# Feed-forward products of a two-layer decoder step: seven block products in place of eight, with the activations kept in DRAM

## The chip, the cores and the metric

The kernel runs on one core of one Trainium2 chip. The metric is device time in microseconds (us) of one execution; smaller is better. TensorE (PE in the profile) multiplies matrices from on-chip memory (SBUF) into PSUM, VectorE (DVE), ScalarE (ACT) and GpSimd (POOL) work element by element, and SyncE (SP) issues most transfers. Each engine takes its own instructions in order.

## The reference

A prompt of 1024 tokens and a group of 64 sample tokens pass through two layers with shared weights, 1088 tokens of 1024 features. Layer 0 mixes tokens by retention and dilated attention, layer 1 by a state-space recurrence with a gated product (GLU). Each layer ends with the same feed-forward part, and that is where the change is made:

```python
def swiglu(h, w_in, w_out):                    # h [tokens, 1024], w_in [1024, 5632], w_out [2816, 1024]
    gate, up = jnp.split(h @ w_in, 2, axis=-1)
    return (jax.nn.silu(gate) * up) @ w_out
...
        yp = yp + swiglu(rms_norm(yp, norm_ffn[layer]), w_ffn_in[layer], w_ffn_out[layer])
```

All arrays are float32.

## The kernel before

Features lie on partitions and tokens along the free dimension, in T = 1092 columns (1088 tokens and 4 empty ones), cut into three parts of CH = 364. Every large product is exact to about float32 by three products of a shortened format: each operand is split into a high part (`split_a`, `split_w`, `w_unit`: an ACT copy) and a low part (a DVE subtraction), and `mm_fm` (line 169 of the profile) adds hi*hi, lo*hi and hi*lo. One output block of 128 features with 8 blocks of input features is 8 x 3 x 3 = 72 matmuls.

`ffn(l, ...)` runs once per layer. It scales and splits the residual `x` into `hh` and `hl`, without the norm's factor; the factor `rb` is multiplied onto the results. Then, for each of the NF = 22 blocks of 128 hidden features, it makes the gate product (72 matmuls), L1223 to L1225 (times the factor, SiLU, times the factor), the up product (72 matmuls), L1234 (the gated activation `a`) and its split. After each pair of blocks `out_proj` multiplies the pair before by its rows of `w_out`: 8 groups of 18 matmuls, each added to `x` by DVE (L1207). So the second product runs between the pieces of the first one, `x` stays in SBUF throughout, and an activation lives only until its pair is used. The last pair is left to `turn_over`: `s5_start` in layer 0, which prepares the state-space layer between the output blocks, and `final` in layer 1, which works by columns of tokens and normalizes the result.

Weights come in units of 256 columns (`w_raw`, 1 MB each, two buffers `raw`).

Beside layer 0's feed-forward runs background work for the state-space layer, `s5_prep2`, a generator of which `ffn` takes 8 steps per block (`next(bgen, None)`). It has 32 passes `hd` of two groups; each is some 30 POOL instructions (L1021 to L1065) with transposes on PE (L1074, L1084), copies on DVE (L1013) and, every fourth pass, a chain of small DVE and ACT instructions (`phases`, L851). Its memory is the pool `prep`, opened above the split activations and held until `eh.close()`. In layer 1 the background is `caches`: sixteen copies of 4080 KB from DRAM to DRAM, issued by POOL.

From the attention on, everything stands in one block whose order on each engine is set when the program is built, by a planner that runs through the instructions on a simulated device (`tc.block(schedule_with_timeline_sim=True)`); the engines then take that order as it is.

## Time and profile before

| what | us |
|---|---|
| median of 3 runs (lowest to highest) | 2705.1 (2701.85 to 2706.35) |
| span of the profiled execution | 2704.3 |
| layer 0's feed-forward, first to last matmul (743.3 to 1579.2) | 835.9 |
| layer 1's feed-forward up to the last gate and up product (1891.1 to 2660.6) | 769.5 |
| PE busy in the whole span | 2630.6 (97%) |

The times of the runs are of the device. The span is from the first to the last instruction of the one execution that was profiled; it lies inside the range of the timed runs, so what stands around it in the timed figure is within a microsecond or two. Busy PE time says that a matmul was under way, not that PE ran at its best rate: the rate is read from how many matmuls a stretch of time holds.

### The profile page before, as it was taken

How to read it: one execution, taken by the hardware profiler on the slowest of the kernel's cores; microseconds unless marked ns; L12 is line 12 of the kernel's file. 1: busy time of each engine (PE TensorE's matmuls, PEld its weight loads, DVE VectorE, ACT ScalarE, POOL GpSimd, SP SyncE). 2: the span in 40 equal slices, each digit the busy share in tenths (PEclk: the TensorE clock that was granted, in tenths of full speed). 3: DMA queues.
4: the chain of work that ended last, by engine and by line, in shares of the span. 5: the costliest groups of instructions: out<-in, count | busy, mean ns of one | idle time of the engine just before them, and what ended most of it. 6: DMA issues, size and time to landing. Idle time of an engine off the chain costs nothing.

```text
span 2704.3 us, 43413 instructions
## 1 busy us (share of the span) xinstructions
PE 2630.6 (97%) x17493; PEld 2514.5 (93%) x17493; DVE 1178.8 (44%) x2224; ACT 739.9 (27%) x1283; POOL 702.1 (26%) x1337
## 2 busy tenths in 40 slices
PE   7999999999999999999999988999999999999998
PEld 7997788778999999999999987999999999999998
DVE  6223333965554444344434368532433333333325
ACT  5113344764232111122111175321311111111112
POOL 2000022431026765666670044300100000000003
PEclk9999999989999999999999999999999999999999
DMA  8337852314133322223326199411565546431001
GB/s 238 121 101 258 289 202 73 83 40 140 59 80 91 92 74 74 71 79 88 88 70 114 50 289 250 140 57 38 173 231 171 169 143 216 156 109 47 32 32 75
DMA packets 258153, 331.52 MB, mean 123 GB/s; under 512 B 59697, under 2 KB 223441, under 8 KB 256673
## 3 DMA queue, kind: packets, MB, share of 16 engines
q1 hardware_dynamic: 254896, 255.58, 31.9%
q0 software_dynamic: 3056, 73.17, 7.9%
q8 instruction: 138, 2.26, 0.4%
q14 instruction: 63, 0.51, 0.1%
HBM read 270.06 MB, written 129.66 MB: 148 GB/s over the span
## 4 chain that ended last, share of the span: by engine, by line
PE 85%; DMA 6%; DVE 5%; ACT 2%; issue 1%; SPq 1%; POOL 1%; DVEq 0%; POOLq 0%; ACTq 0%
PE big L169 64%; PE ch L308 7%; PE ch L215 2%; PE po L729 1%; DMA x_d<-x 1%; DMA kv<-in_state_swa_k 1%; PE tr L718 1%; PE tr L367 1%; PE po L409 1%; DMA U<-h_d 1%; PE sc L702 1%; PE sm L169 1%; DMA out_swa_v_prompt<-v_ev 1%; PE pb L1561 1%; PE sc L374 1%
## 5 line engine op out<-in xcount | busy, mean ns | idle before, releaser
L169 PE MATMUL big<-hh,wh_i 128*128 128x364 f32 (+1 forms) x2080 | 461.4, 329 | 0.9 <-DVE sg L1223 0.9
L169 PE MATMUL big<-hh,wl_i 128*128 128x364 f32 (+1 forms) x2080 | 460.1, 328 | 0.0
L169 PE MATMUL big<-hl,wh_i 128*128 128x364 f32 (+1 forms) x2080 | 458.6, 327 | 0.0
L169 PEld LDWEIGHTS big<-hh,wl_i 128*128 128x128 f32 x2080 | 361.6, 188 | 0.1
L169 PEld LDWEIGHTS big<-hh,wh_i 128*128 128x128 f32 x2080 | 359.5, 188 | 2.3 <-DVE sg L1223 1.2
L169 PEld LDWEIGHTS big<-hl,wh_i 128*128 128x128 f32 x2080 | 358.5, 188 | 0.1
L790 ACT ACTIVATE wh_i<-raw 128x1024 fp32r<-128x1024 f32 x111 | 117.7, 1060 | 868.2 <-PE big L169 825.2
L1207 DVE TENSOR_TENSOR x<-big,x 128x1092 f32<-128x1092 f32 x168 | 217.1, 1293 | 204.4 <-PE big L169 204.4
L1225 POOL TENSOR_TENSOR sg<-sg,ssq 128x1092 f32<-128x1092 f32 x21 | 53.4, 2541 | 806.1 <-ACT sg L1224 806.1
L169 PE MATMUL big<-a_hi,wh_o 128*128 128x364 f32 x1008 | 225.8, 332 | 6.3 <-DVE a L1234 3.5
L169 PE MATMUL big<-a_hi,wl_o 128*128 128x364 f32 (+1 forms) x1008 | 222.8, 329 | 0.0
L169 PE MATMUL big<-a_lo,wh_o 128*128 128x364 f32 (+1 forms) x1008 | 222.1, 328 | 0.0
L1223 DVE TENSOR_TENSOR sg<-big,ssq 128x1092 f32<-128x1092 f32 x44 | 57.0, 1295 | 341.7 <-PE big L169 339.1
L1234 DVE TENSOR_TENSOR a<-big,sg 128x1092 f32<-128x1092 f32 x42 | 54.4, 1295 | 324.8 <-PE big L169 320.9
L169 PEld LDWEIGHTS big<-a_hi,wh_o 128*128 128x128 f32 x1008 | 171.9, 188 | 11.1 <-DVE a L1234 4.1
L169 PEld LDWEIGHTS big<-a_lo,wh_o 128*128 128x128 f32 x1008 | 176.1, 188 | 0.0
L169 PEld LDWEIGHTS big<-a_hi,wl_o 128*128 128x128 f32 x1008 | 174.7, 188 | 0.3 <-issue 0.2
L791 DVE TENSOR_TENSOR wl_i<-raw,wh_i 128x1024 fp32r<-128x1024 f32 x109 | 137.1, 1258 | 50.7 <-ACT wh_i L790 50.7
L126 ACT ACTIVATE wh_o<-raw 128x1024 fp32r<-128x1024 f32 x44 | 46.4, 1060 | 323.9 <-PE big L169 310.7
L308 PE MATMUL ch<-h_hi,wh_a 128*128 128x364 f32 (+1 forms) x384 | 129.3, 337 | 0.3 <-ACT wh_a L121 0.3
L308 PE MATMUL ch<-h_lo,wh_a 128*128 128x364 f32 (+1 forms) x384 | 128.8, 335 | 0.0
L308 PE MATMUL ch<-h_hi,wl_a 128*128 128x364 f32 (+1 forms) x384 | 128.3, 335 | 0.0
(556 smaller groups left out, 4535.1 us busy)
## 6 DMA issues: line engine op xcount, KB each, us to landing
raw<-in_w_ffn_in SPq DMA_DIRECT2D x44, 1024.0 KB
out_swa_k_sample<-in_state_swa_k POOLq DMA_DIRECT2D x8, 4080.0 KB, 15.6
out_swa_v_sample<-in_state_swa_v POOLq DMA_DIRECT2D x8, 4080.0 KB, 15.8
raw<-in_w_ffn_out SPq DMA_DIRECT2D x22, 1024.0 KB
kv<-in_state_swa_k SPq DMA_DIRECT2D x40, 512.0 KB
kv<-in_state_swa_v SPq DMA_DIRECT2D x40, 512.0 KB
raw<-in_w_in_ab SPq DMA_DIRECT2D x24, 512.0 KB
tb<-sc_all SPq DMA_DIRECT2D x16, 642.0 KB
```

The source lines that it names most:

```text
L126: S.activation(hi, src, AF.Copy)
L169: last = PE.matmul(pc[c][:, :n], lhsT=w(k), rhs=a(k, c)[:, :n], start=j == 0, stop=j == K * 3 - 1)
L215: PE.matmul(pv[:n, :256], lhsT=a[:, k, tk], rhs=w[:, k % 4, :], start=j == 0, stop=j == 23)
L308: PE.matmul(pb[:, :n], lhsT=w[:, k], rhs=a[:, k, c * CH:c * CH + n], start=j == 0, stop=j == 23)
L367: PE.transpose(pt[:, hp], kn[:, hp * 128:(hp + 1) * 128], ident)
L374: PE.matmul(ps_[hp * 32:hp * 32 + 32, :w], lhsT=qs[:, hp, b], rhs=kt[:, hp, :w], start=True, stop=True)
L790: S.activation(hi, r, AF.Copy)
L791: split_ins[0] = (eng or V).tensor_tensor(lo, r, f32(hi), op=OP.subtract)
L1207: V.tensor_tensor(c3(x[:, m]), pb[:, :, :CH], c3(x[:, m]), op=OP.add)
L1223: V.tensor_tensor(c3(sg), pg[:, :, :CH], c3(rb), op=OP.mult)
L1225: last_op = (G if l and f < NF - 1 else V).tensor_tensor(sg, sg, rb, op=OP.mult)
L1234: V.tensor_tensor(c3(a), pu[:, :, :CH], c3(sg), op=OP.mult)
```

## The change

The first product is computed by Strassen's scheme, in Winograd's form. A unit is 1024 input features by 256 weight columns. Its weights are a 2 x 2 block matrix (512 x 128 each), and so are the activations (512 features by HT = 544 tokens). Seven products of sums of blocks replace eight products of blocks, for every one of the 44 units per call (22 in each layer). A product is 4 blocks of features x 3 terms x 2 parts of QC = 272 columns = 24 matmuls.

What this moves around it:

- The norm's factor is applied to the activations before the product, so their sums can be formed once per layer; `x` is used up for it and goes to DRAM (`x_d`) before, in halves of tokens, and is loaded again for the second product. The products ahead of each feed-forward part (three of the output projection, the last of the GLU) are done in halves of tokens (`mm_half`), with the norm's sums between them.
- Each unit forms its weight sums and seven splits on DVE and ACT. Results are put together from PSUM by DVE.
- All 22 blocks of gated activations go to DRAM (`a_d`) and come back for the second product, which now follows the whole first one: `out_proj(0, 8)`, `out_proj(8, 15)`, and the rest in `turn_over`.
- Background steps: 8 per unit instead of 8 per block of gate and up.

The core of the diff:

```diff
+    class Halves:      # PSUM: two banks "sm", and either 2 tiles of three banks (big) or 3 of two (pair)
...
+        hc = eh.enter_context(tc.tile_pool(name="ffh", bufs=1, reuse_waits="tile"))
+        H = {}
+        for nm in ("S2", "S3", "S1", "A22", "S4", "A12", "A11"):
+            H[nm] = [hc.tile([128, 4, HT], F32R, name="%s_%s" % (nm, pt)) for pt in ("hi", "lo")]
+        def put(nm, k, src, eng):
+            hi, lo = H[nm]
+            S.activation(hi[:, k], src, AF.Copy)
+            eng.tensor_tensor(lo[:, k], src, f32(hi[:, k]), op=OP.subtract)
+        E = G if l else V
+        class Unit:
+            def split(self, nm, src, hilo=None):
+                hi, lo = hilo or [w4.tile([128, 4, 128], F32R, name=n) for n in ("wh_p", "wl_p")]
+                S.activation(hi, src, AF.Copy)
+                V.tensor_tensor(lo, src, f32(hi), op=OP.subtract)
+            def weights(self, nm):
+                sub = lambda o, a, b: V.tensor_tensor(o, a, b, op=OP.subtract)
+                if nm == "S2":
+                    sub(b11, b12, b11)
+                    self.t2 = tp[0].tile([128, 4, 128], F32, name="t2", bufs=1)
+                    sub(self.t2, b22, b11)
+                elif nm == "S3":
+                    sub(b12, b22, b12)
+                elif nm == "A22":
+                    sub(b21, b21, self.t2)
+                self.split(nm, ...)
+            def prod(self, nm):
+                    for k in range(4):
+                        for w, a in ((hi, ah), (lo, ah), (hi, al)):
+                            for c in range(2):
+                                last = PE.matmul(ps[:, c, :QC], lhsT=w[:, k], rhs=a[:, k, c * QC:(c + 1) * QC], ...)
+            def put(self, j, hf, a, b):
+                if not self.up:
+                    V.tensor_tensor(o, a, b, op=OP.add)
+                    S.activation(o, o, AF.Silu)
+                else:
+                    V.tensor_tensor(t, a, b, op=OP.add)
+                    bgen_after[0] = E.tensor_tensor(o, t, o, op=OP.mult)
+            def m1(self): ...  # A11, copied by ACT     def m2: A12, put    def m6: S2, u2 = p + m1
+            def m7(self): ...  # S3, u3 = p + u2        def m5: S1, u2 = p + u2, put    def m4: A22, put   def m3: S4, put
...
+        def norm(o, k, hf, eng):
+            S.activation(o, o, AF.Identity, scale=g[:, k:k + 1])
+            eng.tensor_tensor(o, o, ssq[:, half(hf)], op=OP.mult)
+        for k in range(4):
+            norm(blk[k][0], k, 0, V)
+            put("A11", k, blk[k][0], V)
...
+        for k in range(4):
+            norm(blk[k][1], k + 4, 0, V)
+            put("A12", k, blk[k][1], G)
...
+        for k, (a11, a12, a21, a22) in enumerate(blk):
+            norm(a21, k, 1, G)
+            norm(a22, k + 4, 1, V)
+        for k, (a11, a12, a21, a22) in enumerate(blk):
+            V.tensor_tensor(q1[k], a21, a22, op=OP.add)
+            G.tensor_tensor(a21, a11, a21, op=OP.subtract)
+            V.tensor_tensor(a11, q1[k], a11, op=OP.subtract)
+            put("S2", k, a11, V)
+        ... # put S3 (G), S1 (V), A22 (V); a12 - a11 (G), put S4 (G)
-        for gi in range(NG):
-            ... # gate, up and, per pair, out_proj
+        for gi in range(NG):
+            for u in (gate unit, up unit):
+                u.m1(); u.m6(); u.m2(); u.m7(); u.m5(); u.m4(); u.m3()
+                if bgen_after[0] or not l:
+                    bg_step(8)
+            pending.append(lambda sg=sg, gi=gi: [SP.dma_start(a_d[:, gi * 2 + j], sg[:, j]) for j in range(2)])
+        for _ in bgen:
+            pass
+        eh.close()
+        def load_a(f, slot):
+            ... # memory of ffw (slots 0 to 5), zp (6, 7), ffw2 (from 8)
+            SP.dma_start(lo[:, :NT], a_d[:, f])
+            G.memset(lo[:, NT:], 0.0)
+            S.activation(hi, lo, AF.Copy)
+            V.tensor_tensor(lr, lo, f32(hi), op=OP.subtract)
+        def out_proj(f0, f1, hook=None):
+            for m in range(KT):
+                wv = w_unit(raw, m % 2, n=f1 - f0)
+                mm_fm(pb, wv, f1 - f0, ...)
+                V.tensor_tensor(c3(x[:, m]), pb[:, :, :CH], c3(x[:, m]), op=OP.add)
+        for f in range(8):
+            load_a(f, f)
+        x = x_tile(xr)
+        for m in range(KT):
+            SP.dma_start(x[:, m], x_d[:, m])
+        f2 = e2.enter_context(tc.tile_pool(name="ffw2", bufs=1, reuse_waits="tile"))
+        for f in range(8, 15):
+            load_a(f, f)
+        out_proj(0, 8)
+        for f in range(15, NF):
+            load_a(f, f - 15)
+        out_proj(8, 15)
+        turn_over(fp, zp, out_proj, outs, acts)
```

Pools of the changed kernel are opened with `reuse_waits="tile"`: a tile waits for the tiles that lay in its place, not for the whole pool. By the tiles' sizes, per partition: the seven splits `H` take 122 KB from the bottom of the pool stack, `prep` lies above them; `ffw`, `zp` and `ffw2` take 131 KB from the same bottom, so that the low parts of blocks 12 to 14 (the top of `ffw2`) lie where `prep` lay.

## Rows read from the trace of the kernel before

**Rows 1.** Windows: us of the stretch, busy us per engine (instructions), granted clock, DMA share

```profile
743.30:1579.20 835.90, 827.36 (x5054) 807.86 (x5054) 359.72 (x448) 179.11 (x269) 438.61 (x1010) 1.00 0.32 87
1891.10:2660.60 769.50, 768.57 (x4646) 768.11 (x4644) 271.75 (x223) 126.60 (x119) 61.26 (x37) 1.00 0.39 130
759.90:1435.80 675.90, 668.89 (x4098) 650.16 (x4097) 287.94 (x379) 135.39 (x225) 420.97 (x992) 1.00 0.29 82
1925.00:2000.00 75.00, 75.00 (x454) 75.00 (x454) 1.00 0.81 270
```

**Rows 2.** PE's waits in layer 0's feed-forward: line, releaser, total us, times, longest

```profile
PE big L169 <- DVE a L1234: 3.5, 2, 2.0
PE sm L1105 <- DMA Ex<-in_state_ssm_im: 1.5, 2, 0.8
```

**Rows 3.** Critical chain, in order of time: start us, us, what

```profile
391.48 23.70 PE ch L215 x198
...
851.59 24.08 PE big L169 x144
...
1669.98 6.43 DMA hz<-z_d
```

**Rows 4.** Lines L272, L1207, L790: durations in ns, min/median/max, and shapes

```profile
L272 DVE TENSOR_TENSOR h_lo<-g,h_hi x9: 431/683/1678, 7.7 to 49.4; 128x512 fp32r<-128x512 f32 x8, 128x272 fp32r<-128x272 f32 x1
L1207 DVE TENSOR_TENSOR x<-big,x x168: 1281/1295/1297, 830.4 to 2643.8; 128x1092 f32<-128x1092 f32 x168
L790 ACT ACTIVATE wh_i<-raw x111: 1041/1062/1066, 643.6 to 2613.1; 128x1024 fp32r<-128x1024 f32 x111
```

**Rows 5.** Line L1225: durations in ns on DVE and on POOL

```profile
L1225 DVE TENSOR_TENSOR sg<-sg,ssq x23: 1283/1328/2254, 773.2 to 2659.2; 128x1092 f32<-128x1092 f32 x23
L1225 POOL TENSOR_TENSOR sg<-sg,ssq x21: 2540/2540/2543, 1922.8 to 2603.7; 128x1092 f32<-128x1092 f32 x21
```

**Rows 6.** Timeline at 889 us, and line L1062 on POOL in ns

```profile
889.48 3.64 POOL L1021 TENSOR_TENSOR u<-Cc,tA 128x144 f32<-128x144 f32 x4
...
889.60 1.39 DVE L791 TENSOR_TENSOR wl_i<-raw,wh_i 128x1024 fp32r<-128x1024 f32 x1
...
890.92 1.52 DVE L1225 TENSOR_TENSOR sg<-sg,ssq 128x1092 f32<-128x1092 f32 x1
...
L1062 POOL TENSOR_TENSOR u<-tE x128: 394/407/1456, 805.7 to 1410.3; 128x128 f32<-128x128 f32 x128
```

**Rows 7.** DVE groups in layer 0's loop (742 to 1510 us): busy us, mean ns

```profile
L791 DVE TENSOR_TENSOR wl_i<-raw,wh_i 128x1024 fp32r<-128x1024 f32 x43 | 56.9, 1323 | 0.3 <-ACT wh_i L790 0.3
L1225 DVE TENSOR_TENSOR sg<-sg,ssq 128x1092 f32<-128x1092 f32 x21 | 29.4, 1400 | 0.5
L127 DVE TENSOR_TENSOR a_lo<-a,a_hi 128x1092 fp32r<-128x1092 f32 x21 | 29.0, 1381 | 6.8 <-ACT a_hi L126 6.7
L127 DVE TENSOR_TENSOR wl_o<-raw,wh_o 128x1024 fp32r<-128x1024 f32 x20 | 25.8, 1294 | 19.4 <-ACT wh_o L126 19.4
```

**Rows 8.** POOL's waits in layer 0's loop: total us, times, longest

```profile
POOL u L1021 <- DVE u L851: 78.2, 7, 20.5
POOL Bp L1036 <- PE sm L1084: 65.3, 7, 18.1
POOL u L1021 <- DVE Cc L1013: 26.5, 3, 13.8
POOL Bp L1036 <- DMA B<-in_ssm_b_im: 15.7, 2, 8.6
```

More of the change, by code (lines that the diff above doesn't have):

```diff
@@ L22 @@
 T = 3 * CH
+HT = NT // 2
+QC = HT // 2
 TP = 1152
@@ new lines, in behind, with norm_stats, norm_rows @@
+    def behind(ins):
+        return tc.issue_after(ins.ins) if ins is not None else ExitStack()
+    def norm_stats(pool, hf, after=None):
+        pr = psX.sm()
+        with behind(after):
+            for i, o in enumerate((0, 128, 256, 384, HT - 128)):
+                last = PE.matmul(pr[:, i:i + 1], lhsT=ssq[:, hf * HT + o:hf * HT + o + 128], rhs=ones, start=True, stop=True)
+        return rstd_newton(pool, pr[:, :5]), last
+    def norm_rows(r, hf, after=None):
+        pa, pb = psX.sm(), psX.sm()
+        with behind(after):
+            for i in range(4):
+                PE.matmul(pa[:, i * 128:(i + 1) * 128], lhsT=r[:, i:i + 1].to_broadcast([128, 128]), rhs=ident, start=True, stop=True)
+            last = PE.matmul(pb[:, :HT - 512], lhsT=r[:, 4:5].to_broadcast([128, 128]), rhs=ident[:, 640 - HT:], start=True, stop=True)
+        S.activation(ssq[:, hf * HT:hf * HT + 512], pa, AF.Copy)
+        S.activation(ssq[:, hf * HT + 512:(hf + 1) * HT], pb[:, :HT - 512], AF.Copy)
+        return last
@@ new lines, in mm_half @@
+    def mm_half(ps, wv, K, ah, al, after=None, mid=None):
+        hi, lo = wv
+        terms = [(w, a, k) for k in range(K) for w, a in ((hi, ah), (lo, ah), (hi, al))]
+        for j, (w, a, k) in enumerate(terms):
+            if mid and j == K * 3 // 2:
+                after = mid(last)
+            with behind(after):
+                for c in range(2):
+                    r = a(k, c)
+                    o = ps[:, c, :QC]
+                    if len(r.shape) == 3:
+                        o = o.rearrange("p (s c) -> p s c", s=8)
+                    last = PE.matmul(o, lhsT=w(k), rhs=r, start=j == 0, stop=j == K * 3 - 1)
+        return last
@@ L1171, in step_kernel @@
             pass
+        raws = first_raws(0)
+        pe = None
+        for hf in range(2):
+            for j, wv in enumerate(last):
+                m = 5 + j
+                pb = psX.big()
+                o = hf * HT
+                pe = mm_half(pb, wv, KT, lambda k, c: m_hi[:, k, o + c * QC:o + (c + 1) * QC], lambda k, c: m_lo[:, k, o + c * QC:o + (c + 1) * QC], pe)
+                if hf and j == 0:
+                    r0, pe = norm_stats(xP, 0, pe)
+                elif hf and j == 1:
+                    pe = norm_rows(r0, 0, pe)
+                xv = x[:, m, half(hf)].rearrange("p (c n) -> p c n", c=2)
+                V.tensor_tensor(xv, pb[:, :2, :QC], xv, op=OP.add)
+                save_half(tC, m, hf)
@@ new lines, in ffn @@
+        t1, t2 = half(0), half(1)
+        g = gains["ffn%d" % l]
+        blk = [[x[:, k + d, t] for t in (t1, t2) for d in (0, 4)] for k in range(4)]
+        def norm(o, k, hf, eng):
[4 more added lines that the diff above has]
+            put("A11", k, blk[k][0], V)
+        first = Unit(0, None, False, raws[0])
+        first.after = first_after
@@ new lines, in ffn @@
+        first.split("A11", first.block(0, 0), [s1.tile([128, 4, 128], F32R, name=n, bufs=1) for n in ("wh_s", "wl_s")])
+        first.m1s = s1.tile([128, 2, QC], F32, name="m1", bufs=1)
+        first.m1()
+        r1, first.after = norm_stats(xP, 1, first.after)
+        first.split("A12", first.block(1, 0), [wU.tile([128, 8, 128], F32R, name=n)[:, :4] for n in ("wh_i", "wl_i")])
+        for k in range(4):
+            norm(blk[k][1], k + 4, 0, V)
+            put("A12", k, blk[k][1], G)
+        p2 = first.prod("A12")
@@ new lines, in ffn @@
+        first.after = norm_rows(r1, 1, first.after)
+        q1 = [s1.tile([128, HT], F32, name="q1") for k in range(2)]
+        q1 += [ssq[:, hf] for hf in (t1, t2)]
+        for k, (a11, a12, a21, a22) in enumerate(blk):
[6 more added lines that the diff above has]
+            put("S2", k, a11, V)
@@ L1324, in hook @@
                     load_t(i)
-        out_proj((NF - 2, NF - 1), hook)
+        out_proj(15, NF, hook)
     U, tabs = {}, {}
```

350 lines of the change are left out of this document (245 added, 105 removed).

## The prediction

> **What bounds the kernel now.** I read the page's busy shares first, then windows over the two feed-forward parts, then the chain of waits inside them. In both parts PE is the limit: it is busy 827.4 of 835.9 us in layer 0 and 768.6 of 769.5 us in layer 1, at the full clock (1.00), while DVE has work for 360 and 272 us and POOL for 439 and 61 us [rows 1]. PE's longest wait for another engine in layer 0 is 2.0 us [rows 2]. So what counts is how long PE takes per matmul. A busy share can't tell that, but a piece of the chain without waits can: 144 matmuls of 364, 364 and 360 columns take 24.08 us, 0.1672 us each, and 198 of 256 columns, every one with new weights, take 23.70 us, 0.1197 us each [rows 3]. The reader is to see that the price goes nearly by columns; the narrower matmul isn't bound by its weight load.
>
> **What the change takes from PE.** Before, a layer's first product is 44 outputs x 72 = 3168 matmuls x 0.1672 = 529.7 us. After, it is 22 units x 7 products x 24 = 3696 matmuls of 272 columns. No row has that width; on the line between the two prices of [rows 3] (0.0475 us for 106.7 columns) it is 0.1268 us, so 468.7 us. The gain is 61.0 us a layer. Bounds: the price of 256 columns (442 us, gain 87), and that price enlarged by 272/256 (470 us, gain 60). I take the line, since 272 lies next to 256. The second product keeps its matmuls: 22 x 72 = 1584 x 0.1672 = 264.8 us, of which 240.8 (20 of 22 blocks) lie in layer 1's window. Check: layer 1 before is 3168 + 1440 = 4608 x 0.1672 = 770 against 769.5 [rows 1]. In layer 0 835.9 - 529.7 - 264.8 leaves 41.4 us: 8.5 us idle, and 33 us of matmuls for the background and the norm, which stay. The five outputs that are now made in halves cost 96 x 0.1268 = 12.2 in place of 12.0 us each, 1 us together.
>
> **What it adds to the other engines.** A subtraction of 512 elements took DVE 0.683 us, one of 1092 from PSUM 1.295 us [rows 4]; on that line 544 elements take 0.72 us. A unit gives DVE 4 weight sums and 7 low parts (11 x 0.683 = 7.5 us), 7 additions from PSUM (5.0 us) and, in layer 0's up units, 4 multiplications (2.9 us): 14.0 us on average per unit, against 168 x 0.1268 = 21.3 us of PE. ACT has 7 high parts at about half of 1.062 us [rows 4], one copy and half the time four SiLUs, about 6 us. Neither is the limit by load, and three PSUM pairs and four weight buffers stand between them and PE. DVE loses 64 of its 88 additions to `x` a layer, hidden before and after.
>
> **Start of each part.** Formerly PE began as soon as one block was split. Now the norm's factor, the sums and seven splits come first. POOL has 24 instructions of 544 elements; scaled from 2.540 us for 1092 [rows 5] each takes 1.27 us, 30.5 us in all. DVE has 36 instructions with both operands in SBUF beside them, and these two kinds don't run together (next part): 36 x (0.72 - 0.2) us, three quarters of them met, add 14 us, so 44 us until S4 is split. PE can do eight products before it needs S4 (A11 and A12 of gate and up, then S2, S3, S1, A22): 24.3 us. That leaves a stall of 20 us per layer; 8 if four products of the up unit go ahead of S4, 32 if the chain starts 12 us late. I take 20.
>
> **Between the products.** Blocks 0 to 7 must come back before `out_proj(0, 8)`. Their memory is that of S2, S3 and S1, which the last unit uses up first, so the loads (6.43 us for 544 KB [rows 3]) can begin some 9 us before its end; what isn't covered is the last additions from PSUM and the split of the first `w_out` block. Bounds 0 and one load with its split, 6.4 + 1.1 + 1.3 = 8.8 us; I take 4. The DRAM traffic itself (12 MB out, 12 MB back, `x` twice 4.5 MB, a layer) lies beside PE at DMA shares of 0.32 and 0.39 [rows 1]. In layer 1 sixteen copies now come one per unit: 4.18 MB + 1.05 MB of weights + 0.56 MB of activations in 21.3 us is 272 GB/s, what a stretch of before carried at a share of 0.81 without holding PE (75.00 of 75 us busy) [rows 1]. I cost it at nothing; if it isn't covered, a weight unit comes late in layer 1 alone.
>
> **Layer 0's background, the term that decides.** When POOL and a DVE instruction with two SBUF operands meet, one waits for the other: at 889 us L791 takes 1.39 us and L1225 1.52 while four POOL instructions take 3.64 us [rows 6]; the DVE groups of this kind run 0.1 us over their undisturbed 1.215 and 1.296 us [rows 7]; L1062 takes 0.407 us in the middle and 1.456 at most [rows 6]. So a meeting costs POOL 1.05 us for an instruction of 1.25: its length less 0.2. (The Trainium skill, SBUF — State Buffer, section "SBUF: two separate sides", calls it an exclusive lock, held for the whole instruction. By whole lengths the delay worked out below would be 140 in place of 99 us and the forecast 2698; the rows show 0.2 us less per meeting.)
>
> Before, the background ran 675.9 us with POOL busy 421 [rows 1]. In it lie waits on PE's order and on loads, 65.3 + 26.5 + 15.7 = 107.5 us [rows 8], and 105 DVE instructions of the kind [rows 7], met with a chance of 421/676, at 1.05 us: 68 us. Without these it is 500 us, 71% of it POOL work; the chains of small instructions (78.2 us [rows 8]) are in it. After, a unit has 11 + 2 such DVE instructions, 8.9 us, which cost 13 x 0.2 less, 6.35 us; 22 units x 6.35 x 0.71 = 99 us. POOL begins 45 us after the start of the part. So the background ends 45 + 500 + 99 + 5 (the second product's splits) = 649 us after the start, though eight steps per unit ask it to be done in 20 units.
>
> Who waits for that? The low parts of blocks 12 to 14 lie in `prep`'s place, and `out_proj(8, 15)` wants them first at 20 + 468.7 + 33 + 10 (DVE late here and there, since POOL now delays it too) + 4 + 96.3 (`out_proj(0, 8)`, 576 matmuls) + 6 = 638 us. They can be there at 649 + 8.8 = 658. PE is held 20 us.
>
> **The sum.** Layer 0: 468.7 + 264.8 + 33 + 20 + 10 + 4 + 20 = 820.5, against 835.9: -15.4. Layer 1: 468.7 + 240.8 + 2 (norm) + 20 + 4 = 735.5, against 769.5: -34.0. With +1: -48 from 2704.3, and 0.8 up to the median: **2657 us**.
>
> **Rivals.**
> (1) The background doesn't hold PE, and the start is covered (8 and 2 us in place of 20 and 4): layer 0 776.5, layer 1 721.5, together -106: 2600. For it: POOL's 107 us of waiting show that it isn't pressed now [rows 8]. Against it: two passes per unit want 2 x 500/32 = 31 us of a unit of 21.
> (2) Slower: PE's order is fixed when the program is built. Its background transposes (L1074, L1084), and SP's stores of POOL's results, stand in that order at the times that the planner gave POOL. If it gave POOL none of the 99 us of meetings, PE and, through weight loads queued behind those stores, its units wait for them within the first product: 2657 + 99 - 20 = 2736. At worst each of 16 units takes two full passes (31 + 4.5 us in place of 22.8): 2657 + 16 x 13 - 20 = 2845. It decides from 48 us, 3 us per unit. For it: POOL is oversubscribed in the new first product even without meetings. Against: before, PE waited for the background 1.5 us in all [rows 2].
> (3) DVE paces the units: 14.0 us of work plus 13 x 0.1 of meetings and some 1.5 of background copies is 79% of a unit in layer 0, in a fixed order, with evictions and next weights in one queue. One to one and a half us uncovered in each of 44 units: 2701 to 2723. Against: in layer 1 its load is 60%.
>
> **How the numbers follow.** The forecast's case has 0.45 (2635 to 2690), rival 1 0.25 (2585 to 2635), rival 2 0.18, rival 3 0.12. A measurement of this kernel tells about 0.2%, 5.4 us, from no change. Faster: 0.45 + 0.25 + half of rival 3 = 0.76; the same: most of the rest of rival 3 and a tail of rival 2, 0.07; slower 0.17. The range goes from 2590 (rival 1 but for its lower end) to 2725 (rival 3 whole, rival 2 left out from there).
>
> **What would show it.** In the changed profile: the first product's matmuls start 0.127 us apart where PE doesn't wait, and 3696 of them a layer; a gap of PE of some 20 us in all within the first 60 us of each feed-forward part, ended by POOL's S3 or S4; the last POOL instruction of the background near 650 us after layer 0's start, and the load of block 12 behind it; DVE waits of 0.1 to 0.3 us per instruction in layer 0 and nearly none in layer 1; layer 1 gaining about twice what layer 0 gains. Wrong would be: PE waiting unit by unit for background or weights (rivals 2, 3), or layers that gain alike (rival 1). The forecast fails most easily in the 500 us of background, from which small changes go into PE's hold one to one.

## The result, and the profile after

The changed kernel takes 2845.4 us (median of 4, 2839.1 to 2848.4), the kernel before 2703.5 beside it (4, 2698.0 to 2706.4): a ratio of 1.053, 95% interval 1.051 to 1.055. It is slower by 142 us, where 48 us less were forecast. Its profiled span is 2837.3 us, 133.0 more than before.

Windows of the changed kernel, columns as in [rows 1], the last one GB/s. In each layer: the first unit (with 20 matmuls of the norm's sums in it); the other 21; the time to the first matmul of the second product; the second product, in layer 0 in two rows (297.0 us together).

```profile
741.30:811.50 70.20, 30.03 (x189) 28.95 (x189) 57.19 (x69) 20.60 (x35) 36.74 (x24) 0.64 0.04 5
811.50:1336.00 524.50, 490.26 (x3754) 469.94 (x3752) 341.64 (x597) 156.75 (x318) 388.01 (x853) 0.98 0.36 107
1336.00:1347.00 11.00, 2.02 (x15) 0.81 (x14) 4.49 (x6) 3.39 (x4) 10.57 (x30) 0.76 0.86 278
1347.00:1451.00 104.00, 97.68 (x561) 94.36 (x562) 27.28 (x22) 18.64 (x29) 56.53 (x128) 0.94 0.71 176
1451.00:1644.00 193.00, 184.92 (x1085) 182.89 (x1084) 56.71 (x48) 50.71 (x49) 15.11 (x20) 0.97 0.49 143
1968.20:2034.10 65.90, 28.89 (x188) 27.81 (x189) 53.03 (x60) 21.33 (x35) 36.14 (x22) 0.68 0.19 65
2034.10:2532.40 498.30, 451.20 (x3530) 450.12 (x3528) 261.85 (x373) 128.91 (x207) 75.56 (x64) 0.95 0.59 204
2532.40:2538.70 6.30, 0.29 (x4) 0.07 (x2) 4.17 (x4) 3.12 (x3) 1.59 (x9) 0.81 0.93 301
2538.70:2795.50 256.80, 244.05 (x1440) 242.89 (x1441) 80.97 (x69) 45.20 (x45) 0.71 (x7) 0.97 0.28 102
```

Against [rows 1], layer 0 takes 902.7 us (741.3 to 1644.0) where it took 835.9, and layer 1 827.3 where it took 769.5. 12 us more lie ahead of layer 1's first matmul, 4 less elsewhere. PE, formerly busy for 99% of layer 0, now stands still or runs at 1.2 GHz at every change of stage.

What a unit costs when nothing stops it is read from experiment e3 below, where layer 1's last 21 units run without a wait:

```profile
2135.30:2578.20 442.90, 442.90 (x3530) 442.88 (x3528) 262.35 (x373) 129.89 (x207) 74.38 (x57) 1.00 0.46 162
```

442.9 / 3528 = 0.1255 us per matmul of 272 columns, 21.09 us per unit; 22 units are 464 us, where the eight products took 529.7. So the scheme gives PE its 65.7 us a layer, and the rest of the stage takes that and 67 or 58 us more. By the prediction's own terms:

| layer 0 | forecast | measured |
|---|---|---|
| 22 units | 468.7 | 464.0 |
| second product and background on PE | 264.8 + 33 | 264.8 + 33 (taken as forecast) |
| start of the part | 20 | 49.1 (70.2 - 21.1) |
| units held | 10 | 57 (524.5 - 442.9 - 25 for 226 of the background's matmuls) |
| between the products | 4 | 11.0 |
| held before blocks 8 to 14 | 20 | 8 |
| loads, background and clock in the second product | 0 | 16 (297.0 - 264.8 - 8 of background - 8) |

| layer 1 | forecast | measured |
|---|---|---|
| 22 units, norm | 470.7 | 464.0 (the norm's 2 stand in the start) |
| second product, 20 blocks | 240.8 | 240.8 |
| start of the part | 20 | 44.8 (65.9 - 21.1), and 12 ahead of it |
| units held | 0 | 55.4 (498.3 - 442.9) |
| between the products | 4 | 6.3 |
| loads late in the second product | 0 | 16.0 (256.8 - 240.8) |

The 25 us are an estimate: 33 us for 302 matmuls in the kernel before, in proportion. In e10 below, where PE hardly waits, its units take 36 us more than 442.9 for 221 matmuls of the background. So of the 57 us 34 are PE's waits (524.5 - 490.3), some 11 the clock, and some 12 the background's own matmuls, which cost more between units than the 25 (11 and 12 go by e10).

The hold of 8 us is PE's wait of 7.2 us at 1465.7 us, ahead of the first product with `f_hi`, and 0.9 behind it. Three terms make most of the loss: the starts, layer 0's units, layer 1's units. PE's waits show each. In the names below, `wh_p` and `wl_p` are the high and the low part of a sum of weights; Sx, Ox and Ex are tables that POOL makes for the background (Cs is one that it loads), and PE transposes or multiplies them (L1118, L1181, L1191). In the two starts (732 to 812 us and 1955 to 2035 us; 35.4 us in each, 4.3 ahead of layer 0's first product, 12.0 ahead of layer 1's):

```profile
PE pp L1377 <- ACT wh_p L1350: 35.4, 1, 35.4
PE pp L1377 <- ACT wh_s L1350: 4.3, 1, 4.3
...
PE pp L1377 <- ACT wh_s L1350: 12.0, 1, 12.0
```

After four products PE waits 35.4 us for S2's weight. The timeline shows what DVE and POOL do then (DVE's first two lines, then POOL's):

```profile
771.12 1.84 DVE L1458 TENSOR_TENSOR ssq<-x,x 128x544 f32<-128x544 f32 x1
772.89 0.71 DVE L1333 TENSOR_TENSOR A_lo<-x,A_hi 128x544 fp32r<-128x544 f32 x1
...
768.87 1.75 POOL L1459 TENSOR_TENSOR x<-x 128x544 f32<-128x544 f32 x1 [0.66 <-DVE q L1458]
770.58 1.81 POOL L1333 TENSOR_TENSOR S_lo<-x,S_hi 128x544 fp32r<-128x544 f32 x1
```

Here they take turns: a DVE instruction of 0.71 us takes 1.84 when it meets one of POOL, and POOL's take 1.75 to 1.81 where the shortest of this shape took 1.33 (L1397 in layer 1). POOL's 24 instructions of the start take 41.5 us in all, meetings included. But POOL waits too (735 to 798 us):

```profile
POOL x L1435 <- ACT ssq L898: 13.4, 1, 13.4
POOL x L1459 <- DVE q L1458: 3.2, 2, 2.5
POOL x L1468 <- DVE x L1460: 2.0, 2, 1.3
POOL x L1459 <- DVE ssq L1458: 0.7, 1, 0.7
```

The 13.4 us (14.6 in layer 1) are for the norm's factor of the second half of the tokens: the matmuls of its sums stand behind PE's first product, at 751 us, and the factor is there at 757, 15.8 us after PE's first matmul. The last low part of S4 is out at 797.0 us, 55.7 after that matmul, and the chain runs to 798, 57 after it. Its last link is the weight sum `t2`, whose place lies in `x`, and so behind the last low part of S4:

```profile
795.74 1.80 DVE L1356 TENSOR_TENSOR t<-raw 128x512 f32<-128x512 f32 x1 [1.88 <-POOL S_lo L1333]
```

PE then goes on at half clock (windows, granted clock third from the end):

```profile
790.00:798.00 8.00, 0.00 (x0) 0.00 (x0) 6.12 (x5) 4.99 (x8) 7.00 (x5) 0.50 0.00 0
798.00:802.00 4.00, 2.75 (x10) 2.44 (x11) 4.00 (x8) 1.77 (x4) 0.00 (x0) 0.50 0.00 0
802.00:806.00 4.00, 4.00 (x21) 4.00 (x20) 1.58 (x3) 0.54 (x1) 0.00 (x0) 0.53 0.00 0
806.00:810.00 4.00, 4.00 (x35) 4.00 (x34) 3.41 (x10) 0.73 (x2) 0.28 (x2) 1.00 0.45 44
```

So a wait costs more than its length: in layer 0's first unit PE is busy for 30.0 us with what takes 21.1 at full clock and with the norm's sums, some 2 us, so some 7 us go to the clock. The 49.1 us are thus 40.2 of waits (35.4, and the rest mostly for low parts of weights), 7 of clock and 2 of the norm.

In layer 0's other units PE waits for the background in its own order (811 to 1336 us), 1.5 us in all before [rows 2]; these are the two largest:

```profile
PE sm L1181 <- POOL Sx L1131: 24.7, 14, 4.0
PE sm L1191 <- POOL Ox L1131: 5.0, 5, 1.6
```

In layer 1's other units PE waits 47.1 us in all (2034 to 2533 us), in two stretches: 14 us between 2095 and 2135 us, half of them for DVE, and 32.9 from 2285 to 2318 for the high part of a weight sum, whose load took from 2274.4 to 2317.8:

```profile
PE pp L1377 <- ACT wh_p L1350: 39.4, 2, 32.9
PE pp L1377 <- DVE sg L1392: 7.7, 1, 7.7
```

POOL's timeline before the first stretch, the critical chain there, and a window:

```profile
2057.99 0.55 POOL L1869 DMA_DIRECT2D out_swa_v_sample<-in_state_swa_v  x1
2058.53 0.50 POOL L1869 DMA_DIRECT2D out_swa_k_sample<-in_state_swa_k  x1
2059.02 0.50 POOL L1869 DMA_DIRECT2D out_swa_v_sample<-in_state_swa_v  x1
```

```profile
2087.00 43.84 DMA raw<-in_w_ffn_in
```

```profile
2094.00:2104.00 10.00, 3.57 (x29) 3.35 (x27) 1.45 (x2) 0.60 (x1) 4.11 (x5) 0.94 1.00 342
```

Three copies of 4.18 MB leave together, and two more at 2099.8 and 2100.4 us: 12.5 MB are 37 us at 342 GB/s, and from 2058 to 2131 us the DMA share is 0.99. The 1 MB of weights issued behind the three takes 43.8 us to land. Before the second stretch three leave at 2249 us and two at 2288. A copy is released by the multiplication of an up unit (`bgen_after`), and the gate unit after it takes its steps with the same, long fulfilled release. So copies come in twos and threes every second unit.

### The profile page after: what moved, and what is told of

It reads as the page before. It is cut to its first block, busy times and chain, and to the rows that moved or that the text cites. A ratio compares the mean times of both kernels' runs of the same rounds, so it can differ in the third digit from the quotient of the medians.

```text
span 2837.3 us, 47758 instructions
## 1 busy us (share of the span) xinstructions
PE 2557.9 (90%) x18677; PEld 2432.8 (86%) x18677; DVE 1456.8 (51%) x2848; ACT 907.6 (32%) x1668; POOL 828.0 (29%) x1436
## 4 chain that ended last, share of the span: by engine, by line
PE 64%; POOL 11%; DMA 9%; DVE 8%; issue 3%; ACT 2%; another core or an unknown queue 2%; SPq 1%; POOLq 0%; DVEq 0%; ACTq 0%
PE big L171 24%; PE pp L1377 19%; PE ch L310 6%; PE ch L217 3%; POOL u L1128 3%; PE big L929 2%; POOL Ex L1170 2%; DMA raw<-in_w_ffn_in 2%; POOL u L1169 2%; POOL u L1168 1%; DMA kv<-in_state_swa_k 1%; PE po L731 1%; PE tr L720 1%; DMA z_lo<-a_d 1%
## 5 line engine op out<-in xcount | busy, mean ns | idle before, releaser
L1377 PE MATMUL pp<-S_hi,wh_p 128*128 128x272 f32 x1408 | 299.6, 294 | 70.8 <-ACT wh_p L1350 70.8
L1377 PE MATMUL pp<-S_hi,wl_p 128*128 128x272 f32 x1408 | 296.7, 292 | 2.5 <-DVE wl_p L1351 2.5
L1377 PE MATMUL pp<-S_lo,wh_p 128*128 128x272 f32 x1408 | 295.4, 291 | 0.0
L1377 PEld LDWEIGHTS pp<-S_hi,wh_p 128*128 128x128 f32 x1408 | 224.2, 191 | 73.3 <-ACT wh_p L1350 71.2
L1351 DVE TENSOR_TENSOR wl_p<-raw,wh_p 128x512 fp32r<-128x512 f32 x260 | 195.1, 752 | 147.3 <-ACT wh_p L1350 147.1
L1377 PE MATMUL pp<-A_hi,wh_p 128*128 128x272 f32 x1024 | 218.7, 295 | 47.9 <-ACT wh_p L1350 40.2
L1377 PEld LDWEIGHTS pp<-S_hi,wl_p 128*128 128x128 f32 x1408 | 226.3, 192 | 3.7 <-DVE wl_p L1351 3.1
L1377 PEld LDWEIGHTS pp<-S_lo,wh_p 128*128 128x128 f32 x1408 | 224.0, 191 | 0.8 <-issue 0.6
L1377 PE MATMUL pp<-A_lo,wh_p 128*128 128x272 f32 x1024 | 217.8, 293 | 0.0
L1377 PE MATMUL pp<-A_hi,wl_p 128*128 128x272 f32 x1024 | 217.1, 293 | 0.2
L1397 POOL TENSOR_TENSOR sg<-cs,sg 128x544 f32<-128x544 f32 x44 | 71.0, 1615 | 436.3 <-ACT wh_p L1350 218.4
```

The costliest lines, as they stand in the source:

```text
L1351: V.tensor_tensor(lo, src, f32(hi), op=OP.subtract)
L1377: last = PE.matmul(ps[:, c, :QC], lhsT=w[:, k], rhs=a[:, k, c * QC:(c + 1) * QC], start=n == 0, stop=n == 11)
L1397: bgen_after[0] = E.tensor_tensor(o, t, o, op=OP.mult)
```

## The experiments

Times of e1 to e10 are single executions, beside 2697.6 to 2704.3 us for the kernel before; the windows carry the verdicts. e11 to e16 have 4 to 7 executions each and a ratio to 7 to 12 of the kernel before. Where layer 1's copies fall changes with the order of the whole program: its other 21 units take 498 to 500 us in the changed kernel, e2, e6, e8 and e10, but 493 in e9 and 482 to 484 in e1, e4 and e7, though none of these edits is about them. So the total of a single run carries up to 17 us that its edit didn't aim at.

**e1, memory for the start**

```diff
-        first.m1s = s1.tile([128, 2, QC], F32, name="m1", bufs=1)
...
+        first.m1s, up_m1 = (s1.tile([128, 2, QC], F32, name="m1", bufs=2) for _ in range(2))
+        first.t2 = s1.tile([128, 4, 128], F32, name="t2", bufs=1)
```

> The first unit's t2 and the first up unit's m1 get memory of their own in place of a place inside x. Theory A (memory): after the change PE stops at the start of each part because the weight sum t2 and the evicted product m1 lie where x lies, so nothing goes on until the last low part of S4 is out (798 us, 57 us after the start). With memory of its own S2's weight is ready early, S2 is multiplied as soon as its halves of H are there, some 10 us before S4's, and the first unit takes 56 to 62 us in place of 70.1 and 65.9: 8 to 14 us per layer, 16 to 28 in all. Rival B (the chain of DVE and POOL alone sets the restart, wherever t2 lies): the first units change by less than 3 us each.

Measured: first units of 66.1 and 61.9 us, 4 less each, between the two theories; 2823.9 us in all; 15 of the 21.5 us lie in layer 1's other units (483.1 us for 498.3), where the copies fell otherwise. PE's waits at the start are now for H itself:

```profile
PE pp L1378 <- ACT S_hi L1332: 20.4, 1, 20.4
PE pp L1378 <- DVE S_lo L1333: 6.8, 2, 6.4
```

The place of `t2` is the last link, but the chain behind it is nearly as long: S2's first high part comes 41 us after PE's first matmul, though PE could use it after four products. S2's sums stand in the middle of the chain.

**e2, the start on DVE alone.** `put`, `norm`, and the differences of the preparation take V where they took G:

```diff
-            norm(a21, k, 1, G)
+            norm(a21, k, 1, V)
...
-            put("S3", k, a21, G)
+            put("S3", k, a21, V)
```

> The 24 instructions per layer that POOL does in the preparation of H's seven sums and splits go to DVE. Theory A (the two engines exclude each other): in the profile after the change a DVE instruction that meets one of POOL takes 1.85 us in place of 0.71, so 24 of POOL's cost DVE about 24 x 1.15 = 27 us of delay and save it 24 x 0.71 = 17; all on DVE, 60 x 0.71 = 43 us in place of 57 from start to restart, and the first unit gets 10 to 14 us shorter in each layer, 20 to 28 us in all. Rival B (the engines work side by side, the chain is what it is by its dependences): DVE has 17 us more to do in the chain, and the first unit gets up to 17 us longer in each layer.

Layer 0's first unit:

```profile
736.80:795.00 58.20, 28.93 (x188) 27.95 (x189) 47.90 (x90) 21.45 (x34) 0.28 (x2) 0.71 0.05 6
```

Measured: 58.2 and 55.8 us, 12 and 10 less; the run 2811.9. Theory A: giving 24 of the 60 instructions to the second engine made the chain longer. From the norm's factor to the last low part of S4 DVE alone takes 29.4 us, both took 39.9.

**e7, both**

> The two edits of the start together: memory of their own for the first t2 and the first up unit's m1, and the whole preparation on DVE. By the runs so far memory alone gave 4 us per first unit (70.1 to 66.1, 65.9 to 61.9), since S2's own halves are not ready before 778 us; DVE alone gave 12 and 10. If the chain on DVE is the bound and the memory matters only behind it (theory A), the two add up or do better, since S2 comes some 6 us earlier with the shorter chain: first units of 50 to 54 and 47 to 52 us. If DVE's chain takes up all that the memory gave (rival B): 58 and 55 us, as with DVE alone.

Measured: 54.6 and 53.7 us, above theory A's ranges, in layer 1 nearer to theory B's figure; 2808.0 in all, 14 of the 37 us in layer 1's other units (484.2). 33 us per layer over a unit remain; the wait for the norm's factor, some 15 us after the first matmul, is in them.

**e3, copies released in gate units too**

```diff
-                    S.activation(o, o, AF.Silu)
+                    bgen_after[0] = S.activation(o, o, AF.Silu)
```

> In layer 1 the 16 copies of 4080 KB are released by the last SiLU of a gate unit as well as by the last multiplication of an up unit; their number and their size stay. Theory A (bursts): released every second unit, two or three copies start together, up to 12.5 MB, about 40 us of what the DMA engines carry (320 GB/s), and the 1 MB of weights that is loaded behind them comes 43 us late, twice. Released one per unit, no PE gap over 5 us is left behind a load of raw weights, and layer 1's units from the second on take 443 to 455 us in place of 498: 43 to 55 us less. Rival B (volume): 4.18 + 1.05 + 0.56 MB in 21.1 us are 274 GB/s with the rows in their present form, too much for loads in time however it is spread; the waits of PE for raw weights sum up to 40 us or more as now, in more and smaller pieces.

The edit did something else. Tied to an ACT instruction, a copy no longer waited in POOL's queue for what releases it: eight of the sixteen ran at 391 us, and PE was held there. Whether the chip or the order set by the build let them go isn't shown.

```profile
400.00:492.00 92.00, 6.88 (x38) 6.47 (x36) 0.00 (x0) 0.47 (x1) 0.00 (x0) 0.55 0.99 332
```

The run took 2886.5 us. Its layer 1, with eight copies, gave the undisturbed price above; it can't tell bursts from volume.

**e5, all sixteen copies, one per unit, by POOL's own instruction**

```diff
                     S.activation(o, o, AF.Silu)
+                    if l:
+                        bgen_after[0] = G.tensor_copy(ssq[:, 1100:1101], self.sg[:, j, hf * HT:hf * HT + 1])
...
-                    bg_step(8)
+                    bg_step(7 if l else 8)
```

> Layer 1 alone is changed: all 16 copies of 4080 KB stay, but POOL now also copies one column of each gate unit's SiLU output, and its queue holds exactly one DMA copy behind each of 16 units, where the changed kernel has two or three behind every second unit. A unit then carries 4.18 + 1.05 + 0.56 MB in 21.1 us, 274 GB/s. Theory A (bursts): no wait of PE for raw weights over 3 us, units from the second on 443 to 450 us in place of 498, the run about 50 us shorter. Rival B (volume): loads come late in many units, PE waits for raw weights 20 to 60 us in sum as now (39 us and the clock's fall), the run within 15 us of the changed kernel.

```profile
2037.10:2484.40 447.30, 444.60 (x3529) 444.41 (x3528) 261.65 (x373) 129.63 (x207) 93.44 (x108) 1.00 0.68 235
```

447.3 us in place of 498.3, PE's longest wait 2.7 us (for DVE, not for a load), the run 2790.9: theory A. The 4.4 us over 442.9 aren't the volume's: with the same sixteen copies, one per unit, e11 to e16 take 443.1 us, as here e13:

```profile
1987.50:2430.60 443.10, 443.10 (x3530) 442.93 (x3528) 262.25 (x374) 129.62 (x207) 93.35 (x108) 1.00 0.68 236
```

So the volume costs nothing to speak of, as the prediction had it; the bursts cost 51 to 55 us.

**e4 and e9, a slower background in layer 0** (`bg_step(8 if l else 6)`, `bg_step(8 if l else 4)`)

> Layer 0's background is issued at six steps per unit in place of eight; the work is the same. Theory A (PE's own order holds its background transposes, and these wait for POOL): PE's 34 us of idle time between 811 and 1336 us end mostly at POOL's Sx, 24.7 us, and the clock's fall behind them costs some 20 more; at six steps a unit asks for 1.4 passes of the background in place of 1.9, near what POOL does, and the units from the second on take 480 to 505 us in place of 525, of which up to 20 us may come back as a wait before blocks 12 to 14 in the second product. Rival B (DVE paces the units): the waits for POOL's Sx are not what sets the unit, and the units stay within 8 us of 525.

> Layer 0's background is issued at four steps per unit in place of eight, about 0.95 passes per unit, some 15 to 17 us of POOL in a unit of 21; the rest comes in the second product. Theory A (units and background wait for each other because two passes per unit are more than POOL does): the units from the second on take 455 to 480 us, and what the background has left runs over into the second product, which is held before blocks 8 to 14 by 40 to 110 us. Rival B (each DVE instruction that meets POOL and each PE instruction of the background costs the unit whatever the pace): per pass the cost stays, the units take 485 to 500 us. In both cases the run as a whole gains little or loses.

At six steps the units took 514.0 us, between the two theories: PE's waits for Sx were gone, but it waited 12.6 us for loads of Cs and 5.6 for Ox. The loads stand in SP's queue behind transfers that wait for POOL. At four steps PE waited little in the units (first row), and the second product lost its cover:

```profile
809.00:1273.00 464.00, 460.01 (x3667) 452.73 (x3667) 313.40 (x532) 144.89 (x275) 256.60 (x559) 1.00 0.34 107
1282.60:1403.00 120.40, 110.73 (x630) 104.56 (x630) 38.89 (x58) 26.77 (x47) 87.46 (x206) 0.94 0.50 166
1403.00:1540.00 137.00, 11.74 (x58) 4.52 (x56) 15.20 (x30) 14.20 (x33) 87.82 (x235) 0.51 0.47 98
```

Units 464.0 us (theory A), then 137 us in which PE, in the middle of the second product, does the rest of the background, 73 of them waiting for Sx, and then waits 43 us for a block. The runs: 2819.5 (16 of the 26 us in layer 1's other units) and 2908.5.

**e6, the background without PE**

```diff
-                PE.transpose(ps_[:, g], Sx[:, g], ident)
...
-            S.activation(So, ps_, AF.Copy)
+            S.activation(So, Sx, AF.Copy)
...
```

One hunk is shown. The edit leaves out the background's other work on PE too (transposes of Cs, the products with Ox) and lets ACT and DVE copy other data in its place, so the results aren't the layer's.

> Left out in layer 0: the background's 8 PE instructions per pass (transposes of Cs and Sx, products of Bp and Ox); ACT and DVE copy other data of the same sizes in their place, POOL's arithmetic and all loads and stores stay. Theory A (PE's order holds work that waits for POOL or for loads queued on SP): PE has nothing left to wait for between the units, the units from the second on take 443 to 460 us in place of 525, of which 25 us are the PE instructions themselves and 55 to 60 the waits and the slower clock behind them. Rival B (DVE's meetings with POOL pace the units): DVE and POOL do what they did, the units lose the 25 us of PE's own work and stay at 490 to 500.

Units 510.7 us: neither. The wait had moved; now ACT stood for POOL, with the next weights' high parts behind it in its queue (ACT's and DVE's waits, 817 to 1328 us):

```profile
ACT So L1177 <- POOL Sx L1128: 105.9, 22, 9.1
...
DVE Cc L1117 <- POOL u L1125: 75.2, 25, 7.2
```

So it isn't PE's order alone: here ACT and DVE, which take steps of the background and of a unit in one queue, held the units as PE had.

**e8, phases ahead of the feed-forward**

```diff
-            if hd % 4 == 2 and hd < 28:
-                phases(hd * 2 + 4)
-                yield
...
+        for g0 in range(0, 64, 8):     # in s5_prep1
+            phases(g0)
+            yield
```

> Layer 0's eight blocks of phases (angles on DVE, sines on ACT, stored to DRAM), of which seven ran within the background of the first product in tiles that POOL's passes use too, are computed before the feed-forward, with tiles of their own; nothing else moves. In the changed kernel POOL stands idle 89.8 of 525 us for DVE's angles in its u tiles, and DVE's angles stand in one queue with the units' evictions and weights. Theory A (the background is late because POOL waits for small instructions that are queued behind units on other engines, and the units in turn wait for it): without them POOL's idle time falls by 60 to 90 us, the last pass ends 50 to 90 us earlier after the start of the part (681 us now), the units from the second on take 470 to 505 us in place of 525, and the hold before blocks 8 to 14 (17 us) goes. Rival B (POOL's arithmetic and its meetings with DVE set the pace): the background ends less than 30 us earlier and the units stay within 10 us.

The background ended 580 us after the start in place of 681, and PE no longer waited before blocks 8 to 14, as A had it; but the units took 549.6 us, longer still, with PE waiting 39.1 us for Sx, and the start waited 29.5 us for the phases:

```profile
PE sm L1199 <- POOL Sx L1149: 39.1, 19, 5.5
```

The run: 2876.6. Theory A fails in the term that counts: with POOL denser the units paid more.

**e10, the tables Ex on DVE** (L1168 to L1172: G to V)

> Layer 0's tables Ex (14 instructions of a pass, 6.5 us on POOL, about 2.8 us on DVE by its rows of 128 elements) go from POOL to DVE. Theory A (POOL's rate sets the units): a pass takes POOL 10 us in place of 16.5, the units from the second on take 465 to 500 us in place of 525 and the background ends 60 us or more earlier. Rival B (DVE's rate and order set the units): DVE gets 1.4 x 2.8 = 4 us more per unit, and the units take 525 to 600 us.

```profile
806.80:1289.00 482.20, 478.80 (x3749) 462.37 (x3748) 394.58 (x946) 154.28 (x309) 211.21 (x458) 1.00 0.39 117
```

482.2 us in place of 524.5, clock 1.00, 3.2 us of waits; 2799.9 in all. DVE is busy for 82% and paces nothing, which rules out rival (3). The second part of theory A failed: the background ended 654 us after the start, only 27 earlier, and the second product took 310.0 us for 297.0, with PE waiting 21.4 for `f_hi`.

**e11, e12, e13, the edits together.** e11 joins e5, e7 and e10 and gives Ex and the phases tiles of their own; e12 is e11 at ten steps per unit; e13 is e11 without those tiles.

```diff
-                v1 = u1[:, 0, :128].rearrange("p (a b) -> p a b", a=8)
...
+                v1, v2 = (p.tile([128, 128], F32, name=nm).rearrange("p (a b) -> p a b", a=8) for nm in ("v1", "v2"))
```

> All that helped, together: the start's memory and its preparation on DVE (2845 to 2808 with both), one copy per unit in layer 1 (to 2791 alone), layer 0's tables Ex on DVE (to 2800 alone), and the tiles that Ex and the phases use on DVE no longer those of POOL's passes, for which POOL stood idle 116 + 112 us when Ex was on DVE. Theory A (three separate causes that add up): 37 + 54 + 46 us off 2845, 2708 us, and up to 20 more if the background now ends early enough for blocks 8 to 14: 2685 to 2712, against 2703 before. Rival B (what one edit frees another takes up again): 2725 to 2770.

> As the kernel with all edits, but layer 0's background at ten steps per unit in place of eight, 2.3 passes: POOL's 10 us a pass come to 23 us in a unit of 22. Theory A (the units wait when the background asks more of POOL than a unit holds): PE waits for POOL's Sx again, units from the second on take 10 us or more longer than with eight, the run 5 to 25 us longer. Rival B (with Ex on DVE the background no longer holds the units at all): units equal within 4 us, the background ends earlier and the run is equal or shorter by what hold was left.

> As the kernel with all edits, but Ex and the phases on DVE use the tiles of POOL's passes again, as with Ex on DVE alone. Theory A (the denser POOL runs, the more often PE, whose order is fixed, meets a transpose or product of the background that isn't ready): with the shared tiles PE waits less than 5 us for the background in the first product of layer 0, the units from the second on take 478 to 490 us in place of 515, the run 2705 to 2722 us. Rival B (the shorter start or layer 1's edit changed layer 0's order, not the tiles): 505 us or more as now, the run within 6 us of 2744.

Layer 0's units in e11, then in e13:

```profile
794.80:1310.00 515.20, 488.48 (x3770) 469.09 (x3768) 445.36 (x998) 156.00 (x322) 224.16 (x497) 0.98 0.38 111
803.00:1286.70 483.70, 478.22 (x3748) 462.04 (x3746) 393.17 (x943) 155.46 (x309) 216.07 (x451) 1.00 0.38 113
```

e11: 2744.3 us, ratio 1.017 (1.015 to 1.019), rival B; layer 0's units 515.2. e12: 2744.1, units 515.1: rival B, the pace asked for no longer matters. e13: 2730.3, ratio 1.011 (1.007 to 1.014), units 483.7 with 5 us of waits, nearly none for the background: theory A for the units; the run 8 us over its range. So the tiles of e11 cost 31.5 us in the units, and why is open: in e13 POOL waits 123 + 109 us for DVE in the shared tiles, but in e11 it waits just as long for ACT, 232 us, and PE then waits 21.6 us in the units for the background, half of it for a copy of DVE's. Added up, the gains of e5, e7 and e10 are 137 us off 2845, of which e13 lacks 22. Some 14 are counted twice, since e7's total holds a gain in layer 1's units that e5 makes too; and the second product of layer 0 took 316 us, 6 more than in e10.

**e14, e15, the second product** (e13 with blocks 6 and 7 loaded where A11 and A12 lay, and layer 0's blocks 8 to 14 in two parts; e15 the same at six steps)

```diff
+        for f in (6, 7, 0, 1, 2, 3, 4, 5):
+            load_a(f, f if f < 6 else f + 2)
...
+            out_proj(8, 12)
+            out_proj(12, 15)
```

> The kernel of the run before, and two edits of the second product: blocks 6 and 7 are loaded into memory of A11 and A12, which the last unit uses first, and layer 0's second part is cut into blocks 8 to 11 and 12 to 14. Theory A (each product's start waits for loads into memory that comes free last): the waits for z_lo and a_hi, 11 + 6 us in layer 1 and about as much in layer 0, fall below 6 us per layer and the wait before blocks 8 to 14, 21 us with Ex on DVE alone, goes: 25 to 45 us less with the clock, the run 2665 to 2690 us. Rival B (the loads queue on SP and the DMA engines behind the last stores wherever their memory lies): 0 to 10 us less.

> The kernel of the run before with layer 0's background at six steps per unit in place of eight. Theory A (PE no longer waits for the background once Ex is on DVE, so its pace sets only when it ends): units within 5 us, blocks 12 to 14 come later, the run equal or up to 20 us longer. Rival B (denser steps still cost the units): the first product of layer 0 10 us or more shorter.

e14 2773.1 us, 1.028 (1.024 to 1.031); e15 2775.2, 1.028 (1.025 to 1.032). In layer 1 theory A holds: the second product takes 241.2 us for its 240.8 (first row), and with the time ahead of it 250 in place of 265. In layer 0 it took 375 us, against 316 in e13: the remaining loads of blocks now left SP's queue only at 1392 us, behind the background's last stores, and PE was busy for 9 of the 97 us of the second row, with waits of 42 for Sx and 41 for a block's high part:

```profile
2489.50:2730.70 241.20, 241.20 (x1440) 241.20 (x1441) 78.17 (x67) 42.73 (x43) 0.71 (x7) 0.99 0.29 104
1309.30:1406.30 97.00, 8.77 (x45) 3.33 (x44) 22.54 (x88) 8.73 (x24) 31.11 (x90) 0.52 0.58 121
```

e15's units took 474.0 us against 482.6 in e14: between its theories.

**e16, seven products in layer 1 alone.** Layer 0's feed-forward is the one before; layer 1 has e5's, e7's and e14's edits.

```diff
-    ffn0 = ffn(0, raws, pe, s5_prep2, s5_start)
+    ffn0 = ffn_eight(raws, s5_prep2, s5_start)
```

> Layer 0's feed-forward is that of the kernel before (eight products, both products interleaved, activations stay on the chip); layer 1 has the seven products with the start's memory, its preparation on DVE, one copy per unit, and blocks 6 and 7 loaded into the memory of A11 and A12. Theory A (the scheme pays by 65 us a layer less some 50 for its start and the changes of product, where nothing else shares the queues with it): layer 1 is 13 us shorter than before, the halves cost 4, the run is 2685 to 2698 us against 2697 to 2703 before. Rival B (what layer 0 leaves behind, its halves and stores, or the state-space stage in its new form costs as much): 2700 to 2720.

Measured: 2692.2 us (7 executions, 2687.6 to 2696.0) against 2701.5 (12, 2696.2 to 2707.9): ratio 0.9965, 95% interval 0.9953 to 0.9978. It is the version that beats both kernels, by 0.35%. Layer 0, the halves, PE's pause ahead of layer 1, its first product, its second:

```profile
736.00:1569.00 833.00, 827.34 (x5038) 807.94 (x5036) 358.17 (x455) 178.05 (x267) 435.63 (x1010) 1.00 0.32 89
1861.00:1888.50 27.50, 27.50 (x212) 27.50 (x211) 13.43 (x26) 8.85 (x14) 0.00 (x0) 1.00 0.20 70
1888.50:1900.50 12.00, 0.48 (x4) 0.24 (x2) 10.44 (x17) 5.61 (x9) 0.00 (x0) 0.63 0.06 23
1900.50:2395.60 495.10, 473.80 (x3716) 472.49 (x3716) 305.53 (x452) 151.18 (x241) 95.25 (x110) 0.97 0.62 214
2404.50:2646.10 241.60, 241.58 (x1440) 241.59 (x1441) 78.33 (x67) 42.73 (x43) 0.71 (x7) 0.99 0.29 103
```

Layer 1 takes 745.6 us (1900.5 to 2646.1) where it took 769.5 [rows 1], and 20 of the 24 are lost again between the layers (331.5 us for 311.9), 12 of them in the pause. The profile is 14.9 us shorter all the same: 2.9 in layer 0's feed-forward and 7.3 ahead of it, where nothing was changed (layer 0's first matmul stands at 736.0 us for 743.3; in other runs' profiles between 736.8 and 746.5), and 0.4 at the end. So some 4 us are the seven products' own, and the 0.35% as a whole can't be put down to them.

## Why the prediction was wrong

**What bounds the kernel, and what the change takes from PE**: right. 0.1268 was forecast, 0.1255 measured, and the gain was 65.7 us a layer for 61.0.

**Start of each part**: the first step that failed, 20 us per layer against 49 and 57 with the pause. Two terms were mis-sized. The chain was put at 44 us and ended after 56: POOL's own work, meetings included, came near (41.5 us), but its wait of 13 to 15 us for the norm's factor was in no term. The prediction's 32 us, for a chain that starts 12 us late, stood beside its choice of 20 as a bound. (The Trainium skill, SBUF — State Buffer, section "SBUF: two separate sides", says that the other engine is blocked for the whole instruction; here 1.84 - 0.71 = 1.13 us of POOL's 1.33, again 0.2 less, so the rule wasn't at fault.) And PE could do four products, not eight: the places of `t2`, `m1` and `sg` in `x` hold the rest, and without them (e1) PE waits for S2, whose sums stand in the middle of the chain. The places alone were worth 4 us (e1), the sharing with POOL 10 to 12 (e2), both 12 to 16 (e7). The clock, not counted at all, added 6 to 7.

**Between the products**: 11.0 and 6.3 us for 4; in range in layer 1 (bound 8.8), not in layer 0.

**Layer 0's background, the term that decides**: its end was forecast at 649 us after the start and came at 681; the blocks behind it were wanted at 717 rather than 638, since all before them was late, so the hold was 8 us for 20. It wasn't the term that decides. What failed is the choice against rival (2): the background holds PE within the units too. They took 57 us over their price where 10 were allowed, 34 of them waits, some 11 the clock and some 12 the background's own matmuls. "Before, PE waited for the background 1.5 us in all" [rows 2] was the wrong witness: it told of a part in which eight steps came in 38 us (835.9 / 22), not in 21. Rival (2) had the mechanism but too narrowly: it named PE's order and SP's (e4), and the chain runs through ACT's and DVE's as well (e6). That the planner misjudged the meetings, as the rival supposed, was not tested by itself; that POOL's pace against the code's order decides is shown by e9 and e10, which relieve POOL, on one side, and by e8, which makes it denser, on the other. e11 and e13 show only that the choice of tiles matters.

**Layer 1's DMA, costed at nothing**: the size was right (443.1 us against 442.9 in e11 to e16), the premise "sixteen copies now come one per unit" wrong. They came in twos and threes, and cost 55 us. The text named the sign, "a weight unit comes late in layer 1 alone".

The total, 2845, equals rival (2)'s worst figure by chance: of its mechanism only a part of the 57 us in layer 0 is there.

Not settled: why separate tiles for the background cost 31.5 us (e11, e13); where the 16 us of layer 0's second product lie in full (PE waits 5.7 us for `z_lo`, 3.9 for `a_hi`, 4.4 for the background's Ox, the rest is put down to the clock), and whether layer 0 could be won by putting its loads into another queue, which was not tried.

## What to carry to other kernels

A saving on the busiest engine is worth its size only while nothing else is made to start, finish or fit in the shortened stage: add up the starts, the changes of product and the background per unit of the new length before the gain. Background work can hold the foreground through each in-order queue that both use (here PE's, SP's, ACT's and DVE's), and making it denser made that worse here (e8); check how far ahead of its program order the slowest engine runs. Releases bundled per pair turn an affordable average into bursts, so look at when transfers leave, not only at their GB/s.

## What the hardware showed unexpectedly

Two engines sharing a chain of instructions with SBUF operands were slower than one: 60 instructions of 544 elements on DVE alone took 10 to 12 us less than 36 on DVE and 24 on POOL. PE's clock was 1.00 until the 35 us stop (763 us), 0.50 from 766 us to its end, and 0.53 in 802 to 806 us, with PE busy throughout that window, before it was 1.00: some 7 us lost at layer 0's start, 6 at layer 1's. And sixteen copies of 4.18 MB delayed a load of weights of 1 MB to 43.8 us when three left together, and cost PE next to nothing when they left one per unit (443.1 us for 442.9).
